# Filter spectra of a long convolution: two half-row products with a sum and a difference on GpSimd, in place of two stacked products

## The chip, the cores and the metric

The kernel runs on one core of a Trainium2 chip. The metric is the device time of one execution in microseconds; the time before is 1944.95 us, the median of three runs that went from 1944.28 to 1946.02 us. A core has TensorE (PE; its weight loads are shown apart as PEld), VectorE (DVE), ScalarE (ACT), GpSimd (POOL) and SyncE (SP, which here issues most DMAs). Each engine takes its instructions strictly in the order in which they stand in its own queue. They meet only through semaphores.

## The reference, cut to what matters

The program is a two-layer block followed by another two-layer block, 256 tokens by 1024 channels in float32. The change touches one piece of the last layer, the filters of a two-sided long convolution and their spectra:

```python
def hyena_filters(l, w1, b1, ..., freq, filt_out):
    ...
    hdn = jnp.sin(fr * (hdn @ w3.astype(f32) + b3.astype(f32)))          # 256 x 64
    h = (hdn @ filt_out.astype(f32)).reshape(l, 2, HY_ORDER, D_MODEL)    # direction, order, channel
    window = jnp.exp(-t.reshape(l, 1, 1, 1) * deltas) + HY_SHIFT
    return h * window

def long_conv(z, h_fwd, h_bwd, skip):
    l = z.shape[1]
    k = jnp.concatenate([h_fwd, jnp.zeros_like(h_fwd[:1]), jnp.flip(h_bwd[1:], axis=0)], axis=0)
    y = jnp.fft.irfft(jnp.fft.rfft(z, n=2 * l, axis=1) * jnp.fft.rfft(k, axis=0)[None], n=2 * l, axis=1)[:, :l]
    return y + z * skip.astype(jnp.float32)
```

The kernel needs the spectrum of `k` only through two combinations of the windowed filters: the even part, forward plus backward, whose cosine transform is the real part, and the odd part, forward minus backward, whose sine transform is the imaginary part. The backward filter counts from its second row on. The skip is added to the first row of the even part.

## The kernel before

Nearly all of the time goes into weight products in three passes: a weight unit `w` of 128x1024 is loaded, ACT rounds it to `wh` (L469), DVE makes the rest `wl` (L470), and TensorE runs three products for each piece (L483 to L485). The filters are side work that has no dependence on the tokens. The generator `filters` (L2032) computes them in eight steps, one for each of two orders `n` and four quarters `q` of 256 channels, and puts the spectra into the DRAM tile `spec` for the last layer.

Before the first step, `hd`, the 64x256 output of the small network, is copied into two 128-row tiles: `he` holds it twice, `ho` holds it above its negative. The backward column of the first row is zeroed in `he`. One step then

- loads the window `fwin`, the skip `fk` and the filter weights `fw`, in which the forward weights stand in rows 0 to 63 and the backward weights in rows 64 to 127,
- makes the even part with `he` and the odd part with `ho`, each as two products of 128 rows by 128 columns against 256 columns (L2061) into a bank of PSUM called `mm`, and multiplies each with the window on DVE into `fb` (L2064); the sum over 128 rows adds or subtracts the two directions,
- adds the skip to one row of the even part on POOL (L2066),
- makes four products with the transform matrix `H` (L2071), two for the even rows of time (j = 0) and two for the odd rows (j = 1), copies the first pair to `fe` on ACT (L2075), and makes `fs` as their sum and `fe` as their difference on DVE (L2077, L2078), which two DMAs write to `spec`.

In float32 each of these products appears in the trace as two passes. All tiles of a step have one buffer, so a step's `fb` is free only when the step before has read it. There are three `mm` banks, and two banks `aux2`.

In the code, six steps stand after the heads of the second block's first layer and ahead of its output projection `ab_w_out` (`self.fill(FILL)`, where one of the seven items is the set-up), and two stand in the ffn of that layer with `aux2` banks. But the program is built with a list scheduler (`schedule_with_timeline_sim=True`), which sets the order of every queue by its own estimates. It moves the six steps forward among the work of the two recurrent heads there: the inverse of the delta rule (L1712 to L1742) and its state scan (L1779 to L1822, states `dS`, output `do`), and the gates and scan of the gated linear attention (L1321 to L1462, output `lo`). Behind those scans `head_out` follows: squares on ACT (L1856), an inverse root `rsq` on POOL from `oss` (L332), the scaling of `do` and `lo` on DVE (L1866), transposes on TensorE (L1875), a product with the gate on DVE (L1877) and the split into `ydh`, `ydl` and `ygh`, `ygl`. The stream of `ab_w_out` reads those four.

Of the kernel before, what the change touches and what calls it, by code (L numbers as in the profile page):

```python
# [10 lines left out]
F32 = mybir.dt.float32  # L11
# [3 lines left out]
AF = mybir.ActivationFunctionType  # L15
OP = mybir.AluOpType
# [3 lines left out]
S = 256  # L20
# [228 lines left out]
class K:  # L249
# [1782 lines left out]
    def filters(self, lp):  # L2032
# [1 line left out]


        nc, A = self.nc, self.A
        he, ho = self.hd2
        for t in (he[:64], he[64:], ho[:64]):
            nc.sync.dma_start(t, self.hd)
        nc.vector.memset(he[64:, 0:1], 0.0)  # L2040
        nc.scalar.activation(ho[64:], self.hd, AF.Copy, scale=-1.0)
        nc.sync.dma_start(self.Hm, A["dft_h"])
        yield
        fo = A["hy_filt_out_2"][0]
        sh = [128, 2, 256]
        for n in range(2):
            for q in range(4):
# [3 lines left out]
                sk = lp.tile([128, 256], F32, tag="fk", name="fk")[0:1, :]  # L2051
                nc.sync.dma_start(sk, A["hy_skip_2"][0, n:n + 1, q * 256:(q + 1) * 256])
                wt = lp.tile([128, 256], F32, tag="fw", name="fw")
                for dr in range(2):
                    c0 = dr * 2048 + n * 1024 + q * 256
                    nc.sync.dma_start(wt[64 * dr:64 * dr + 64, :], fo[:, c0:c0 + 256])
                eo = []
                for i in range(2):
                    ps = self.mm()
                    for m in range(2):  # L2060
                        nc.tensor.matmul(ps[:, m * 256:(m + 1) * 256], self.hd2[i][:, m * 128:(m + 1) * 128], wt,  # L2061
                                         start=True, stop=True)
                    t = lp.tile(sh, F32, tag=f"fb{i}", name="fb")
                    nc.vector.tensor_tensor(t, ps.rearrange("p (m n) -> p m n", m=2), win, OP.mult)  # L2064
                    if i == 0:
                        nc.gpsimd.tensor_tensor(t[0:1, 0, :], t[0:1, 0, :], sk, OP.add)  # L2066
                    eo.append(t)
                for j in range(2):
                    ps = self.mm()
                    for i, t in enumerate(eo):  # L2070
# [135 lines left out]
    def run(self, stages=("b1l0", "b1l1", "b2l0", "b2l1", "fin")):  # L2206
# [18 lines left out]
        if "b2l1" in stages:  # L2225
            fm = es.enter_context(self.pool("fm", "right"))
            self.Fm = fm.tile([128, 512], F32, name="F")
            self.Gm = fm.tile([128, 4, 128], F32, name="G")
            self.Hm = fm.tile([128, 512], F32, name="H")
            self.hd2 = [fm.tile([128, S], F32, name=f"hd{i}") for i in range(2)]  # L2230
            self.spec = self.dr.tile([128, 4, 4 * 512], F32, name="spec")
        if "b2l0" in stages:
            if "b1l1" not in stages:
# [39 lines left out]
```

## Time and profile before

| | |
|---|---|
| median of three runs | 1944.95 us |
| profiled execution | 1944.3 us |
| its span in the trace | 1942.5 us |
| PE busy | 1905.6 us, 98% of the span |
| DVE busy | 1479.6 us, 76% |
| ACT busy | 1050.7 us, 54% |
| POOL busy | 119.0 us, 6% |
| mean granted clock of TensorE | 0.994 |

The span is the time between the first and the last instruction in the trace; 1.8 us of the execution lie outside it. Busy time is the union of an engine's instructions. PE runs its passes into one another, so the distance between the starts of two passes, not the length of one, says how fast it goes. The granted clock is the share of its 2.4 GHz that TensorE was given: 1.0, or 0.5 for 1.2 GHz.

### The profile page before, as it was taken

To read this page: it belongs to the slowest core of one execution; us is meant where nothing else is said; L and a number is where in the kernel's file an instruction comes from. 1 tells how busy PE (TensorE), PEld (TensorE's weight loads), DVE (VectorE), ACT (ScalarE), POOL (GpSimd) and SP (SyncE) were. 2 spreads that over 40 slices of the span, in tenths; PEclk is the share of its full clock that TensorE was granted. 3 is DMA by queue.
4 is the path that set the end of the run, shared out by engine and by line. 5 is a ranking of instruction groups with operands and counts; after the bars stand their busy time and mean duration, and the time that the engine had idled before them with its cause. 6 is when DMAs were issued, how large, how long until landed. Compare 5 with 4: busy or idle time off the path is not lost.

```text
span 1942.5 us, 39726 instructions
## 1 busy us (share of the span) xinstructions
PE 1905.6 (98%) x16234; PEld 1859.7 (96%) x16234; DVE 1479.6 (76%) x2362; ACT 1050.7 (54%) x1642; POOL 119.0 (6%) x120
## 2 busy tenths in 40 slices
PE   7999999999999999999999999998999999999998
PEld 7999999999999999999999999997899999899998
DVE  5988987896776879977778966887775557997554
ACT  6664455564644774454555544765254446555443
POOL 0102000110001001000000000000110000010001
PEclk9999999999999999999999999999999999999999
DMA  8865755966567766756653536443146666535653
GB/s 314 290 220 196 243 188 184 308 237 215 182 226 240 266 213 206 242 166 212 244 186 117 188 115 209 150 152 112 63 153 203 195 189 208 178 112 188 193 190 123
DMA packets 118759, 379.63 MB, mean 195 GB/s; under 512 B 18755, under 2 KB 28784, under 8 KB 117296
## 3 DMA queue, kind: packets, MB, share of 16 engines
q1 hardware_dynamic: 117808, 376.44, 57.7%
q8 instruction: 127, 2.08, 0.4%
q0 software_dynamic: 768, 0.66, 0.1%
q14 instruction: 56, 0.46, 0.1%
HBM read 365.94 MB, written 10.25 MB: 194 GB/s over the span
## 4 chain that ended last, share of the span: by engine, by line
PE 88%; DVE 4%; ACT 3%; issue 2%; DMA 1%; POOL 0%; SPq 0%; DVEq 0%; POOLq 0%; ACTq 0%
PE mm L485 23%; PE mm L483 23%; PE mm L484 23%; DVE wl L470 1%; ACT wh L469 1%; PE mm L519 1%; PE aux L1224 1%; PE mm L520 1%; PE mm L521 1%; PE aux L2123 1%; PE aux L2106 1%; PE aux L859 1%; DMA mw<-in_t_mod_w 1%; PE aux L483 1%; PE aux L485 1%
## 5 line engine op out<-in xcount | busy, mean ns | idle before, releaser
L469 ACT CAST wh<-w 128x1024 fp32r<-128x1024 f32 (+2 forms) x570 | 589.0, 1035 | 626.9 <-PE mm L484 473.6
L470 DVE TENSOR_TENSOR wl<-w,wh 128x1024 fp32r<-128x1024 f32 (+2 forms) x570 | 684.4, 1202 | 280.3 <-ACT wh L469 277.7
L483 PE MATMUL mm<-hh,wh 128*128 128x256 f32 (+1 forms) x1776 | 499.9, 282 | 1.4 <-ACT bq L766 0.7
L485 PE MATMUL mm<-hh,wl 128*128 128x256 f32 (+1 forms) x1776 | 499.4, 282 | 1.2 <-DVE wl L470 1.0
L484 PE MATMUL mm<-hl,wh 128*128 128x256 f32 (+1 forms) x1776 | 498.5, 281 | 0.0
L485 PEld LDWEIGHTS mm<-hh,wl 128*128 128x128 f32 (+1 forms) x1776 | 332.6, 187 | 4.1 <-DVE wl L470 1.8
L483 PEld LDWEIGHTS mm<-hh,wh 128*128 128x128 f32 (+1 forms) x1776 | 332.7, 187 | 3.5 <-issue 1.0
L484 PEld LDWEIGHTS mm<-hl,wh 128*128 128x128 f32 (+1 forms) x1776 | 332.3, 187 | 2.4 <-issue 1.8
L485 PE MATMUL mm<-xh,wl 128*128 128x256 f32 x960 | 269.6, 282 | 1.5 <-DVE wl L470 1.5
L483 PE MATMUL mm<-xh,wh 128*128 128x256 f32 x960 | 267.9, 280 | 1.2 <-DVE dqT L1262 0.7
L484 PE MATMUL mm<-xl,wh 128*128 128x256 f32 x960 | 268.6, 281 | 0.2
L485 PE MATMUL mm<-ph,wl 128*128 128x256 f32 x704 | 196.4, 279 | 0.0
L483 PE MATMUL mm<-ph,wh 128*128 128x256 f32 x704 | 195.9, 278 | 0.0
L484 PE MATMUL mm<-pl,wh 128*128 128x256 f32 x704 | 195.8, 278 | 0.0
L485 PEld LDWEIGHTS mm<-xh,wl 128*128 128x128 f32 x960 | 181.1, 189 | 5.1 <-issue 2.6
L483 PEld LDWEIGHTS mm<-xh,wh 128*128 128x128 f32 x960 | 180.8, 189 | 4.1 <-issue 2.7
L484 PEld LDWEIGHTS mm<-xl,wh 128*128 128x128 f32 x960 | 180.6, 189 | 2.9 <-issue 2.2
L1218 DVE SCALAR_TENSOR_TENSOR macc<-mw,cs,macc 128x512 f32<-128x512 f32 x196 | 145.6, 747 | 14.0 <-DMA mw<-in_t_mod_w 13.1
L484 PEld LDWEIGHTS mm<-pl,wh 128*128 128x128 f32 x704 | 132.4, 188 | 0.0
L485 PEld LDWEIGHTS mm<-ph,wl 128*128 128x128 f32 x704 | 132.2, 188 | 0.1
L483 PEld LDWEIGHTS mm<-ph,wh 128*128 128x128 f32 x704 | 132.1, 188 | 0.0
L483 PE MATMUL mm<-brh,wh 128*128 128x256 f32 x384 | 107.9, 281 | 0.0
(705 smaller groups left out, 3478.6 us busy)
## 6 DMA issues: line engine op xcount, KB each, us to landing
w<-in_t_w_in SPq DMA_DIRECT2D x148, 512.0 KB
w<-in_t_ffn_w SPq DMA_DIRECT2D x128, 512.0 KB
mw<-in_t_mod_w SPq DMA_DIRECT2D x96, 512.0 KB
w<-in_t_ffn_w_up SPq DMA_DIRECT2D x88, 512.0 KB
w<-in_t_ab_w_in SPq DMA_DIRECT2D x42, 512.0 KB
w<-in_t_ffn_w_down SPq DMA_DIRECT2D x40, 512.0 KB
w<-in_t_w_lift SPq DMA_DIRECT2D x32, 512.0 KB
w<-in_t_hy_w_in SPq DMA_DIRECT2D x24, 512.0 KB
```

Of the source, the lines that this page charges most:

```text
L469: nc.scalar.copy(wh, w)
L470: nc.vector.tensor_tensor(wl, w, wh, OP.subtract)
L483: nc.tensor.matmul(ps, wh, xh, start=start, stop=False)
L484: nc.tensor.matmul(ps, wh, xl, start=False, stop=False)
L485: nc.tensor.matmul(ps, wl, xh, start=False, stop=stop)
L519: nc.tensor.matmul(o, h, wh, start=(k + tb == 0), stop=False)
L520: nc.tensor.matmul(o, h, wl, start=False, stop=False)
L521: nc.tensor.matmul(o, l, wh, start=False, stop=(k == KT - 1 and tb == 1))
L859: nc.tensor.matmul(ps[:, jj * S:jj * S + ns], qr[r, 2 * jp + jj, tb * 128:(tb + 1) * 128], kr[r, 0, :ns], start=True, stop=True)
L1218: nc.vector.scalar_tensor_tensor(acc, v[:, k, :], sc, acc, op0=OP.mult, op1=OP.add)
L1224: nc.tensor.matmul(ps[:, m:m + 1], acc[:, m * 128:(m + 1) * 128], self.ones[:, :1], start=True, stop=True)
L2106: nc.tensor.matmul(ps, self.Fm[:, c0:c0 + 128], zt[:, part, :], start=True, stop=True)
```

## The change

In each step the two directions are computed apart. The forward rows of `fw` meet rows 0 to 63 of `he`, the backward rows meet rows 64 to 127, in turns (`m` outside, `r` inside), each into a PSUM bank of its own. Both banks are multiplied with the window. Then POOL makes the difference into a new tile `fo`, the sum in place, and the skip as before. `ho` and what filled it (one DMA, one ACT instruction) go away.

```diff
-        he, ho = self.hd2
-        for t in (he[:64], he[64:], ho[:64]):
+        he = self.he
+        for t in (he[:64], he[64:]):
             nc.sync.dma_start(t, self.hd)
         nc.vector.memset(he[64:, 0:1], 0.0)
-        nc.scalar.activation(ho[64:], self.hd, AF.Copy, scale=-1.0)
...
-                eo = []
-                for i in range(2):
-                    ps = self.mm()
-                    for m in range(2):
-                        nc.tensor.matmul(ps[:, m * 256:(m + 1) * 256], self.hd2[i][:, m * 128:(m + 1) * 128], wt,
+
+                fb = []
+                pd = [self.mm() for _ in range(2)]
+                for m in range(2):
+                    for r in range(2):
+                        p = slice(64 * r, 64 * r + 64)
+                        nc.tensor.matmul(pd[r][:, m * 256:(m + 1) * 256], self.he[p, m * 128:(m + 1) * 128], wt[p, :],
                                          start=True, stop=True)
-                    t = lp.tile(sh, F32, tag=f"fb{i}", name="fb")
+                for r, ps in enumerate(pd):
+                    t = lp.tile(sh, F32, tag=f"fb{r}", name="fb")
                     nc.vector.tensor_tensor(t, ps.rearrange("p (m n) -> p m n", m=2), win, OP.mult)
-                    if i == 0:
-                        nc.gpsimd.tensor_tensor(t[0:1, 0, :], t[0:1, 0, :], sk, OP.add)
-                    eo.append(t)
+                    fb.append(t)
+                odd = lp.tile(sh, F32, tag="fo", name="fo")
+                nc.gpsimd.tensor_tensor(odd, *fb, OP.subtract)
+                eo = [fb[0], odd]
+                nc.gpsimd.tensor_tensor(eo[0], *fb, OP.add)
+                nc.gpsimd.tensor_tensor(eo[0][0:1, 0, :], eo[0][0:1, 0, :], sk, OP.add)
                 for j in range(2):
```

The scheduler also orders the queues anew. Line numbers shift: L2061 becomes L2062, the window product L2064 becomes L2066, difference, sum and skip on POOL are L2069, L2071 and L2072, the products with `H` L2071 become L2076, the copy L2075 becomes L2080, and sum and difference on DVE L2077 and L2078 become L2082 and L2083. In the rows that follow, numbers tell buffers apart; the two directions of a step write different `mm` banks, so two numbers in turns are two row halves in turns.

On PE, the fourth step's products among the scan of the delta rule. Before, the fifth step's products at the same place of the scan:

```order
L2061 MATMUL mm_17047<-fw_17044,hd0_14869 128x256 x2
L1392 MATMUL aux_16670<-lf_16634 128x64 x4
L1392 MATMUL aux_16671<-lf_16634 128x64 x4
L2061 MATMUL mm_17053<-fw_17044,hd1_14870 128x256
L1806 MATMUL aux_15978<-du0_15946,dkd_15945 128x128 x4
```

Now, the fourth step's:

```order
L2076 MATMUL mm_17006<-fo_16998,H_14868 128x256
L2062 MATMUL mm_17022<-fw_17019,hd_14869 128x256 x2
L1806 MATMUL aux_15977<-du0_15945,dkd_15944 128x128 x4
L1779 MATMUL aux_15986<-dS1_15953,dkT_15171 128x128 x4
L1788 MATMUL aux_15996<-dS1_15953,dqT_15316 128x128 x4
L1406 MATMUL aux_16681<-lla_16608,cst_72 128x256 x2
L2062 MATMUL mm_17023<-fw_17019,hd_14869 128x256 x2
L1800 MATMUL aux_16002<-drhs_15991,dY_15192 128x128 x4
```

The scheduler has pulled the turns apart: both products of one direction stand together, and work of the whole array stands between the directions. So it is in steps four, seven and eight; in steps three and six the directions follow each other as two blocks of two; only in steps one, two and five do they stand in turns, as the code writes them.

On PE, the last stretch ahead of the stream of `ab_w_out` (L483 to L485 with `ydh`). Before, from the end of the scans (L1437, L1439) through the transposes of `do` and `lo` (L1875):

```order
L1437 MATMUL aux_16739<-lS1_16697,le31_16619 128x256
L1439 MATMUL aux_16739<-lv_16390,lAT1_16648 128x128 x2
L1875 MATMUL aux_16183<-cst_72,do_15951 128x128
L1875 MATMUL aux_16254<-cst_72,do_15951 128x128
L1875 MATMUL aux_16183<-cst_72,do_15951 128x128 x3
L1875 MATMUL aux_16254<-cst_72,do_15951 128x128 x3
L1875 MATMUL aux_16828<-cst_72,lo_16692 128x128
L1875 MATMUL aux_16899<-cst_72,lo_16692 128x128
L483 MATMUL mm_17100<-ydh_16094,wh_17102 128x256
```

Now, from the last two transposes of `lo` on; the four products of the fifth step (in turns) stand directly behind the last L1439, ahead of the transposes of `do`:

```order
L1875 MATMUL aux_16827<-cst_72,lo_16691 128x128 x3
L1875 MATMUL aux_16898<-cst_72,lo_16691 128x128 x3
L2076 MATMUL mm_17070<-fb_17062,H_14868 128x256
L2076 MATMUL mm_17070<-fo_17066,H_14868 128x256
L2076 MATMUL mm_17074<-fb_17062,H_14868 128x256
L2076 MATMUL mm_17074<-fo_17066,H_14868 128x256
L2062 MATMUL mm_17090<-fw_17087,hd_14869 128x256 x2
L2062 MATMUL mm_17091<-fw_17087,hd_14869 128x256 x2
L2076 MATMUL mm_17104<-fb_17096,H_14868 128x256
L2076 MATMUL mm_17104<-fo_17100,H_14868 128x256
L2076 MATMUL mm_17108<-fb_17096,H_14868 128x256
L2076 MATMUL mm_17108<-fo_17100,H_14868 128x256
```

All products of the fifth and sixth step, which stood among the scans, now stand between the scans and the stream, whose first L483 is the next row. In the sixth step the products with `H` follow the products that they need with nothing between.

On POOL, the same place. Before, from the last memset of the inverse to the squares of the next norm (L364):

```order
L1690 MEMSET dT 128x1024
L2066 TENSOR_TENSOR fb<-fb,fk 1x256 x6
L332 TENSOR_TENSOR rsq<-oss,cst 128x4 x4
L364 TENSOR_TENSOR sq<-sq 128x256 x5
L332 TENSOR_TENSOR rsq<-ms,cst 128x2
```

Now, from the fourth step's skip on, with the numbers:

```order
L2072 TENSOR_TENSOR fb_17028<-fb_17028,fk_17017 1x256
L332 TENSOR_TENSOR rsq_16104<-oss_16095,cst_72 128x4
L332 TENSOR_TENSOR rsq_16115<-oss_16095,cst_72 128x4
L2069 TENSOR_TENSOR fo_17066<-fb_17062,fb_17064 128x512
L332 TENSOR_TENSOR rsq_16753<-oss_16746,cst_72 128x4
L332 TENSOR_TENSOR rsq_16761<-oss_16746,cst_72 128x4
L2071 TENSOR_TENSOR fb_17062<-fb_17062,fb_17064 128x512
L2072 TENSOR_TENSOR fb_17062<-fb_17062,fk_17051 1x256
L2069 TENSOR_TENSOR fo_17100<-fb_17096,fb_17098 128x512
L2071 TENSOR_TENSOR fb_17096<-fb_17096,fb_17098 128x512
L2072 TENSOR_TENSOR fb_17096<-fb_17096,fk_17085 1x256
```

The fifth step's difference stands between the two pairs of inverse roots of `head_out`, the rest of steps five and six behind them. On DVE, the fifth step's two window products (L2066) stand between the scalings of the two halves of `do` (L1866); its sum and difference and the sixth step's window products follow behind the last split of `head_out`.

## Rows read from the trace of the kernel before

**Rows 1.** The page: span; busy time, share, instructions; the chain that ended last.

```profile
span 1942.5 us, 39726 instructions
PE 1905.6 (98%) x16234; PEld 1859.7 (96%) x16234; DVE 1479.6 (76%) x2362; ACT 1050.7 (54%) x1642; POOL 119.0 (6%) x120
...
PE 88%; DVE 4%; ACT 3%; issue 2%; DMA 1%; POOL 0%; SPq 0%; DVEq 0%; POOLq 0%; ACTq 0%
```

**Rows 2.** Windows: stretch, its us, PE, PEld, DVE, ACT, POOL busy, clock, DMA.

```profile
1315.50:1397.00 81.50, 75.15 (x774) 66.22 (x772) 58.73 (x123) 31.84 (x61) 4.41 (x6) 0.96 0.30 97
1321.00:1327.90 6.90, 5.72 (x34) 4.31 (x31) 4.57 (x7) 6.26 (x9) 0.58 (x1) 0.51 0.40 117
1397.00:1405.40 8.40, 4.45 (x20) 3.52 (x19) 6.90 (x18) 5.45 (x24) 4.31 (x4) 0.65 0.00 0
1405.40:1409.80 4.40, 4.40 (x22) 4.40 (x21) 2.89 (x6) 1.24 (x2) 0.00 (x0) 0.50 0.02 4
1409.80:1470.00 60.20, 59.95 (x483) 58.86 (x483) 46.11 (x69) 35.04 (x59) 7.84 (x8) 1.00 0.55 170
```

**Rows 3.** Lines of a step: duration ns min/median/max, first and last start, form.

```profile
L2061 PE MATMUL mm<-fw,hd x48: 378/379/634, 1315.5 to 1379.1; 128*128 128x256 f32 x48
L2064 DVE TENSOR_TENSOR fb<-mm,fwin x12: 652/682/692, 1320.1 to 1380.3; 128x512 f32<-128x512 f32 x12
L2066 POOL TENSOR_TENSOR fb<-fb,fk x8: 711/717/2040, 1320.9 to 1458.4; 1x256 f32<-1x256 f32 x8
```

**Rows 4.** Timeline of PE: start, us, line, array rows*columns, shape, passes [idle before].

```profile
1324.50 2.93 PE L2071 MATMUL mm<-fb,H 128*128 128x256 f32 x6 [1.18 <-ACT osg L1870]
...
1350.81 1.89 PE L2071 MATMUL mm<-fb,H 128*128 128x256 f32 x8
1352.54 1.03 PE L2061 MATMUL mm<-fw,hd 128*128 128x256 f32 x4
```

**Rows 5.** The same; the first row is a window of 0.03 us alone.

```profile
1336.32 0.33 PE L1392 MATMUL aux<-lf 64*128 64x64 f32 x2
...
1336.32 1.11 PE L1392 MATMUL aux<-lf 64*128 64x64 f32 x16
1337.36 1.13 PE L2071 MATMUL mm<-fb,H 128*128 128x256 f32 x4
1338.42 1.06 PE L1718 MATMUL aux<-dT,dY 64*64 64x32 f32 x15
```

**Rows 6.** A POOL group by line and form: count, busy us, mean ns, idle before.

```profile
L1690 POOL MEMSET dY<- 128x2048 f32 x2 | 3.6, 1812 | 21.3 <-PE mm L484 11.4 <-PE aux L1558 9.9
```

**Rows 7.** Timelines of POOL and DVE beside each other; then two lines of DVE.

```profile
1416.35 0.75 POOL L364 TENSOR_TENSOR sq<-sq 128x256 f32<-128x256 f32 x1 [13.25 <-ACT sq L361]
1420.62 1.89 POOL L364 TENSOR_TENSOR sq<-sq 128x256 f32<-128x256 f32 x2 [3.52 <-ACT sq L361]
...
1420.93 1.86 DVE L396 SCALAR_TENSOR_TENSOR ul<-xT,gains,uh 128x256 fp32r<-128x256 f32 x2
...
L396 DVE SCALAR_TENSOR_TENSOR ul<-xT,gains,uh x24: 471/754/969, 1167.7 to 1751.9; 128x256 fp32r<-128x256 f32 x24
L1506 DVE TENSOR_TENSOR ivt<-ivw x28: 412/420/427, 1074.0 to 1311.2; 128x256 f32<-128x256 f32 x28
```

**Rows 8.** Timelines from the scans to the stream: PE, then DVE, then POOL.

```profile
1396.45 0.61 PE L1439 MATMUL aux<-lv,lAT 128*128 128x128 f32 x4
1399.51 0.62 PE L1875 MATMUL aux<-cst,do 128*128 128x128 f32 x2 [2.45 <-DVE do L1866]
...
1405.40 0.56 PE L484 MATMUL mm<-ydl,wh 128*128 128x256 f32 x1
...
1398.67 0.69 DVE L1866 TENSOR_TENSOR do<-do,rsq 128x512 f32<-128x512 f32 x1
...
1400.46 0.69 DVE L1866 TENSOR_TENSOR do<-do,rsq 128x512 f32<-128x512 f32 x1
...
1398.91 2.29 POOL L332 TENSOR_TENSOR rsq<-oss,cst 128x4 f32<-128x4 f32 x2 [0.72 <-ACT ojunk L1856]
```

More of the change, by code (lines that the diff above doesn't have):

```diff
@@ L2229, in run @@
             self.Hm = fm.tile([128, 512], F32, name="H")
-            self.hd2 = [fm.tile([128, S], F32, name=f"hd{i}") for i in range(2)]
+            self.he = fm.tile([128, S], F32, name="hd")
             self.spec = self.dr.tile([128, 4, 4 * 512], F32, name="spec")
```

## Prediction

> **What bounds the kernel now.** I read the page first. PE is busy 98% of the span and holds 88% of the chain that ended last [rows 1]; the weight stream sets the pace, and side work counts where it takes PE's time or keeps PE waiting. The windows show the one place where that differs. From 1315.5 us, the first filter product, to 1397.0, the end of the scans, PE is busy 75.15 of 81.50 us. From 1397.0 to 1405.4 it is busy 4.45 of 8.40 us: the outputs of the heads wait for squares, inverse roots and scalings. From 1405.4 on PE never waits, but until 1409.8 the granted clock is 0.50, and only then 1.00 [rows 2]. So a filter step inside the scans fills PE there, and whatever stands between the last scan product and the stream pushes all that follows.
>
> **Products of the two directions.** A pass of the whole array against 256 columns takes (1352.54 - 1350.81)/8 = 0.216 us at full clock [rows 4], although each one's listed length, with its tail, is 379 ns [rows 3]. Eight passes, 1.73 us, make both directions of a step. With 64 rows, the trace shows that two passes on different row halves run beside each other: in L1392, whose code writes the halves in turns, two start within 0.03 us, and 16 passes take 1337.36 - 1336.32 = 1.04 us, eight pairs of 0.13 [rows 5]. In turns a step would thus take about 4 x 0.216 = 0.86 us and save 0.86. Against it stand the changes between whole and half array: four whole passes between half ones take 1338.42 - 1337.36 = 1.06 us in place of 0.86 [rows 5], so a way there and back costs 0.20, one change 0.10.
>
> But the order of the queues gives turns only in steps one, two and five. Steps one and two, with one extra change each, save 0.75 each. Step three in blocks overlaps only where the blocks meet, 0.216 - 0.10 = 0.1. Step four stands in two places among whole-array work, saves nothing and pays 0.40. Up to the end of the scans this makes 0.75 + 0.75 + 0.1 - 0.4 = **1.2 us** saved. Steps seven and eight, split in the same way inside the weight stream, lose 0.40 each, **0.8 us**. Here the Trainium skill (TensorEngine Tiling (Array Packing), Theoretical Speedup) speaks of up to 2x for a contraction of 64 or less. By that alone eight steps would give 8 x 0.86 = 6.9 us; by the rows and the order the eight save less than 1 us outside the tail.
>
> **Sum and difference on POOL.** No row of before has a 128x512 sum there. One of 128x256 takes 0.75 us, two in a row 1.89 [rows 7]; the skip, one partition by 256, takes 0.717 [rows 3], so columns set the price, not partitions. Doubled, 0.75 gives 1.50 at most. A memset grows by 1.81 us over 2048 columns [rows 6], 0.23 us for 256 more: 0.96 at least. I take 1.35, nearer to the sum, since that has two inputs. A step's chain on POOL was 0.72 and becomes 1.35 + 1.35 + 0.72 = **3.4 us** (2.6 to 3.7). Two of DVE's L396 beside two POOL sums took 1.86 us where one alone takes 0.47 [rows 7]: DVE instructions with two inputs from SBUF wait for the POOL instruction to end, and POOL waits for them, so each of the new sums can hold DVE up by as much as 1.35. The skill (GPSIMD Engine Reference, 4.1 Engine selection) sends an elementwise pair to VectorE, GpSimd being about twice as slow with two inputs; 0.75 against 0.42 for L1506 agrees [rows 7]. By that rule the pair would cost 2 x 0.68 on DVE, and each exposed chain would be 1.3 us shorter.
>
> **The stretch of the scans.** Before, all six steps stood in it; now four do. Two steps of 8 + 8 passes leave: 32 x 0.216 = 6.9 us. With the 1.2 us saved, the scans could end 8.1 us earlier if PE sets their pace. It does mostly (75.15 of 81.50, rows above), but the removed filler also covered the scan's own chain (product, copy, product, update), and the eight new sums of steps one to four hold up DVE, whose part of the chain they can meet. I take **-7** (bounds -8.1 and -4.5).
>
> **From the scans to the stream.** Set the end of the last L1439 to 0, 1396.9 us in before; the stream then began at 8.5 [rows 8]. Now, step by step:
> - Half of `do` is scaled by 2.46 (1398.67 + 0.69) [rows 8]. Then DVE makes the fifth step's two window products, 2 x 0.68 [rows 3]; POOL's difference of 1.35 follows, ahead of two inverse roots. `head_out` is pushed by up to 2.7; DVE waited 1400.46 - 1399.36 = 1.1 us for ACT and POOL in the same place [rows 8], which absorbs part, so 1.6 to 2.7 remain. Two passes of the stream, 0.2 each (22 in 4.40 us [rows 2]), no longer stand among the transposes, which then end at 8.5 + 1.6 - 0.4 = 9.7 to 10.8. I take 10.5.
> - The fifth step's `H` products, eight passes: 1.73 us at full clock, or 0.43 each and 3.46 at half clock; six in 2.93 us, with the tail, at clock 0.51 show that [rows 2, 4]. PE idles in pieces here as it did before, where the clock fell, so I take 3.46.
> - The sixth step's products, one block after the other, seven passes long where the blocks meet: 1.5 us, or 3.0 at half clock. Beside them DVE makes `fs` and `fe` (each as long as a window product), then the window products, the last of them behind the last pass: 4 x 0.68 = 2.7, or 3.0 + 0.68 = 3.7, which I take.
> - POOL's chain with PE waiting: 3.4 (2.6 to 3.7).
> - The sixth step's `H` products: 1.73 to 3.46; I take 3.46, after 3 to 5 us of idle PE.
>
> Sum: 10.5 + 3.46 + 3.7 + 3.4 + 3.46 = 24.5, bounds 9.7 + 1.73 + 2.7 + 2.6 + 1.73 = 18.5 and 10.8 + 3.46 + 3.7 + 3.7 + 3.46 = 25.1. The stream begins **16.0** us later behind the scans (10.0 to 16.6). It lost 2.2 us to the clock before (4.40 us at 0.50); part of this loss now falls on the `H` products, so I give back 0.7 (0 to 2.2).
>
> **The two steps in the ffn.** Besides the 0.8 us of array changes, the `H` products stand some 70 passes behind their inputs, 8 us, and the chain there (window product, 3.4 on POOL, waits of up to 1.2 for each wl on DVE) takes 5 to 9. DVE is busy 46.11 of 60.20 us there [rows 2], with a margin. I take 1.3 in all (0.5 to 4).
>
> The removed ACT instruction and DMA lie far ahead of this, where ACT and the queue have slack: 0. On SP, the sixth step's two stores to `spec` wait longer and stand ahead of one weight load, which itself waits for a buffer that the stream frees: 0.
>
> **Sum.** -7 + 16.0 - 0.7 + 1.3 = +9.6 us. The profiled execution took 1944.3, 0.65 below the median; by the median, 1944.95 + 9.6 = 1954.55, **1954.6 us**. Ends: -8.1 + 10.0 - 2.2 + 0.5 = +0.2, and -4.5 + 16.6 + 4 = +16.1.
>
> **Rivals.**
> - *The clock stays at 1.00 through the tail* (not slower). The products of step five, the transposes and the fifth `H` products now stand where PE idled for 2.45 us; if that keeps the clock up, `H` products and blocks take 1.73, 1.5 and 1.73, and the stream needs no recovery: 10.5 + 1.73 + 2.7 + 3.4 + 1.73 - 8.5 = 11.6 later, less 2.2, less 7.5, plus 0.8 = +2.7, 1947.6. For it: the fall before came only after more than two idle microseconds. Against: PE still waits three times in the tail. It decides where the stream begins before 21 us at full clock. Chance 0.20.
> - *PE sets every price* (faster): the two directions overlap wherever they stand beside other work, DVE fills early and the sixth chain hides behind `head_out`. Then 8 x 0.56 (0.86 less three changes) saved gives 1940.5. The 2x above would be this case. Against it stands the order, in which nothing is between the sixth step's products. Chance 0.06.
> - *DVE becomes the bound in the ffn*: 6.8 us of POOL work there hold DVE, which is busy for three quarters, and late weight splits stop PE for 5 us more: 1959.5. Chance 0.12. The forecast itself has 0.62.
>
> **How the numbers follow.** About 0.2%, 3.9 us, is what a measurement of this kernel can tell from no change. Slower by more: forecast and DVE case, 0.74. Within: the clock rival, 0.20. Faster: 0.06. The range runs from the low end of the sum to its high end, 1945 to 1961; outside it lie the faster case and part of the extremes.
>
> **What would show it.** Right: L1439 ends near 1390, the first `ydh` product of the stream near 1415; PE waits over 4 us ahead of the last four L2076, released by POOL; the clock is 0.5 at the sixth step; L2062 shows overlapping starts only in steps one, two and five. Wrong: POOL's 128x512 sums well under 1 us; a clock of 1.00 between 1395 and 1415; scans that end at 1396 as before, since then the scan's own chain sets their pace and I am too low; or waits at L2076 of the ffn.

## The result, and the profile after

The changed kernel takes 1968.84 us (median of four runs, 1967.2 to 1971.0); the kernel before, beside it, 1945.49 (1944.28 to 1948.18). The ratio is 1.0113, with an interval of 1.0100 to 1.0126: it is 23.4 us slower. I had said slower, by 9.6 us, in a range that ended at 1961: the sign was right, the size and the range were not. The profiled execution took 1971.0 us.

The page of the changed kernel, with the same columns as [rows 1]:

```profile
span 1968.9 us, 39753 instructions
PE 1916.9 (97%) x16234; PEld 1867.5 (95%) x16234; DVE 1489.4 (76%) x2362; ACT 1050.5 (53%) x1641; POOL 143.9 (7%) x136
...
PE 88%; DVE 4%; ACT 3%; issue 2%; DMA 1%; POOL 0%; SPq 0%; DVEq 0%; POOLq 0%; ACTq 0%
```

The page hardly differs. PE is busy 11 us longer in a span that is 26 us longer; POOL, which got 24 us of sums, still shows 7%. To find the loss one has to go by stages. Four marks cut the program: the first filter product, the last L1439 (the end of the scans), the start of the weight stream, the end of PE's work. (Before, two passes of the stream already stand among the transposes, from 1403.6 us on; the mark is its unbroken run from 1405.4 on.) Each stretch against that of the kernel before:

| stretch | before, us | after, us | difference | predicted |
|---|---|---|---|---|
| start to first filter product | 1315.5 | 1320.8 | +5.3 | 0 |
| to the end of the scans | 81.4 | 85.4 | +4.0 | -7 |
| to the stream | 8.5 | 25.4 | +16.9 | +16.0 |
| stream to the end | 530.2 | 530.1 | -0.1 | -0.7 + 1.3 |

The first line is most likely scatter and not the change: ahead of the first filter product the work differs only by the one ACT instruction and the one DMA that filled `ho`. In the changed kernels below this product started between 1316.9 and 1321.1 us, and in the two other kernels that still fill `ho` at 1319.3 and 1320.1. The other three lines add up to +20.8 us of the 23.4. The third came 0.9 us above the forecast, just beyond its upper bound of 16.6. The fourth is 0.7 below, less than this stretch scatters by. The second is where the forecast failed, by 11 us.

The windows of that stretch in the changed kernel, cut where the granted clock changes (columns as in [rows 2]; the last but two is the clock):

```profile
1320.79:1326.46 5.67, 2.27 (x40) 1.71 (x39) 5.23 (x11) 5.59 (x10) 0.00 (x0) 1.00 0.53 181
1326.46:1346.94 20.48, 18.58 (x195) 16.55 (x192) 12.42 (x17) 9.10 (x14) 4.62 (x3) 0.50 0.13 40
1346.94:1367.40 20.46, 16.89 (x270) 14.65 (x268) 16.98 (x28) 8.98 (x16) 7.14 (x6) 1.00 0.34 103
1367.40:1374.25 6.85, 5.61 (x28) 4.96 (x30) 3.31 (x8) 0.00 (x0) 0.12 (x1) 0.50 0.11 41
1374.25:1406.20 31.95, 30.85 (x220) 27.81 (x218) 20.73 (x54) 6.76 (x19) 3.25 (x3) 1.00 0.17 55
sum 85.41, PE 74.19 PEld 65.68 DVE 58.67 ACT 30.43 POOL 15.13; mean PE 14.84 PEld 13.14 DVE 11.73 ACT 6.09 POOL 3.03
```

The same stretch before, and its one window at 0.50:

```profile
1315.49:1396.90 81.41, 75.06 (x774) 66.22 (x772) 58.64 (x123) 31.75 (x60) 4.41 (x6) 0.96 0.30 97
1321.05:1327.88 6.83, 5.65 (x32) 4.24 (x29) 4.55 (x7) 6.21 (x9) 0.53 (x1) 0.50 0.40 118
```

Before, that window was 6.83 us with PE busy 5.65. Now there are two, 20.48 and 6.85 us, with PE busy 18.58 + 5.61 = 24.2. At half clock, half of the busy time is loss: 2.8 us before, 12.1 now, **+9.3**. PE stood idle 81.4 - 75.1 = 6.3 us before and 85.4 - 74.2 = 11.2 now, **+4.9**. What is left, PE's work as it would be at full clock, fell from 72.2 to 62.1 us, **-10.1**. Together +4.1, which is the +4.0. The split is good to about 1 us: a kernel below with the same work on PE shows -9.0 by it. So the work that I wanted out of the stretch, 8.1 us, did leave it; the clock and the waiting took more than it gave.

Where the waits are, from the timeline of PE (start, us, line, shapes, passes, and in brackets the idle time before and who ended it):

```profile
1328.07 0.81 PE L1380 MATMUL aux<-le,le2w 64*128 64x128 f32 x4 [1.21 <-DVE le L1360]
...
1336.40 1.97 PE L1392 MATMUL aux<-lf 64*128 64x64 f32 x16
1338.30 1.22 PE L2076 MATMUL mm<-fb,H 128*128 128x256 f32 x2
...
1368.64 2.07 PE L1779 MATMUL aux<-dS,dkT 128*128 128x128 f32 x8 [4.32 <-DMA dS<-std]
```

Two things are to be seen. The first `H` products of step one stand at 1338.3, 17.5 us behind the step's first product, with some 10 us of half- and quarter-array work (64 rows) ahead of them; before, they began 6.6 us behind it, the last six passes at [rows 4], and the clock rose just behind those. And the scan of the delta rule waits 4.32 us for its first state `dS`; the clock's second fall comes within that wait. The queue of SP shows what stands ahead of its load:

```profile
1361.38 0.37 SPq L2086 DMA_DIRECT2D spec<-fs  x1
1362.10 0.37 SPq L2086 DMA_DIRECT2D spec<-fe  x1
1362.64 1.11 SPq L2055 DMA_DIRECT2D fw<-in_hy_filt_out  x2
1363.86 0.52 SPq L2048 DMA_DIRECT2D fwin<-in_window  x1
1364.56 0.82 SPq L1768 DMA_DIRECT2D dS<-std  x2
```

The state loads stand behind the stores of step two and the loads for step four. What the queue waited for between 1352 and 1366 us, the view of its waits says (us in total, times, longest; its largest entry):

```profile
SPq L2086 <- DVE fs L2082: 4.4, 1, 4.4
```

It waited 4.4 us for DVE's sum `fs` of step two, which ended at 1361.35; from then on it issued one DMA behind the other. The window tile `fwin` has a single buffer, but DVE had read it for step three by 1363.3, before its load had its turn at 1363.9, and the view lists no wait of that load. In the kernel before, the same two state loads were issued here, ahead of the filter's loads:

```profile
1356.07 0.84 SPq L1768 DMA_DIRECT2D dS<-std  x2
1357.01 0.47 SPq L2056 DMA_DIRECT2D fw<-in_hy_filt_out  x1
```

Counted from the first filter product, the first state load is issued at 40.6 us before and at 43.8 now. Of these 3.2 us, 1.9 are the filter's loads ahead of it; the rest is that the stores themselves come later.

### The profile page after: what moved, and what is told of

Its sections match the earlier page's. It is cut to its first block, busy times and chain, and to the rows that moved or that the text cites. A ratio compares the mean times of both kernels' runs of the same rounds, so it can differ in the third digit from the quotient of the medians.

```text
span 1968.9 us, 39753 instructions
## 1 busy us (share of the span) xinstructions
PE 1916.9 (97%) x16234; PEld 1867.5 (95%) x16234; DVE 1489.4 (76%) x2362; ACT 1050.5 (53%) x1641; POOL 143.9 (7%) x136
## 4 chain that ended last, share of the span: by engine, by line
PE 88%; DVE 4%; ACT 3%; issue 2%; DMA 1%; POOL 0%; SPq 0%; DVEq 0%; POOLq 0%; ACTq 0%
PE mm L485 23%; PE mm L483 23%; PE mm L484 23%; PE mm L519 1%; PE mm L520 1%; PE mm L521 1%; DVE wl L470 1%; ACT wh L469 1%; PE aux L1224 1%; PE mm L2076 1%; DMA mw<-in_t_mod_w 1%; PE aux L2128 1%; PE aux L2111 1%; PE aux L859 1%; PE aux L483 1%
## 5 line engine op out<-in xcount | busy, mean ns | idle before, releaser
L483 PE MATMUL mm<-hh,wh 128*128 128x256 f32 (+1 forms) x1776 | 500.6, 282 | 1.4 <-ACT bq L766 0.7
L485 PE MATMUL mm<-hh,wl 128*128 128x256 f32 (+1 forms) x1776 | 500.1, 282 | 1.6 <-DVE wl L470 1.5
L485 PEld LDWEIGHTS mm<-hh,wl 128*128 128x128 f32 (+1 forms) x1776 | 333.3, 188 | 4.5 <-DVE wl L470 2.6
L483 PEld LDWEIGHTS mm<-hh,wh 128*128 128x128 f32 (+1 forms) x1776 | 333.4, 188 | 3.4 <-issue 1.0
L485 PE MATMUL mm<-xh,wl 128*128 128x256 f32 x960 | 268.8, 281 | 1.5 <-DVE wl L470 1.5
L483 PE MATMUL mm<-xh,wh 128*128 128x256 f32 x960 | 267.6, 280 | 1.1 <-DVE dqT L1262 0.7
L485 PE MATMUL mm<-ph,wl 128*128 128x256 f32 x704 | 196.6, 279 | 0.0
L483 PE MATMUL mm<-ph,wh 128*128 128x256 f32 x704 | 196.0, 278 | 0.0
L485 PEld LDWEIGHTS mm<-xh,wl 128*128 128x128 f32 x960 | 181.0, 189 | 4.9 <-issue 2.6
L483 PEld LDWEIGHTS mm<-xh,wh 128*128 128x128 f32 x960 | 180.7, 189 | 3.9 <-issue 2.7
L485 PEld LDWEIGHTS mm<-ph,wl 128*128 128x128 f32 x704 | 132.2, 188 | 0.2
L483 PEld LDWEIGHTS mm<-ph,wh 128*128 128x128 f32 x704 | 132.1, 188 | 0.0
L483 PE MATMUL mm<-brh,wh 128*128 128x256 f32 x384 | 107.9, 281 | 0.0
```

What stands on the lines that cost most here:

```text
L483: nc.tensor.matmul(ps, wh, xh, start=start, stop=False)
L485: nc.tensor.matmul(ps, wl, xh, start=False, stop=stop)
```

## The experiments

My theory after this reading: the tail is what I forecast (two steps deferred, POOL's chain open before PE); the 11 us in the scans are (a) a longer half clock, because the early whole-array products are gone, and (b) the state loads, which a filter load in front of them now holds up. The rivals: half-row products are dear by themselves; POOL's latency alone is all of it; the scans are bound by their own chain. The experiments ran on other chips than the first runs. There the kernel before took 1948.9 to 1950.7 us (medians), and the time of one kernel scattered by 5 us and more, so ratios go against the kernel before on the same chip, and the stretches of the traces, which repeat far better, decide.

**The changed kernel again.** No edit; the base of the others.

> The changed kernel itself, on the chip of the other experiments, as their base. Theory: 18 to 24 us above the kernel before, with the stretch from first filter product to last L1439 near 85 us, a wait of 4 us at L1779 on dS, a half clock of 20 us early in the scans and the stream 25 us behind them. If chance made the first profile what it was, one of the three long items (20 us half clock, 4 us wait, 25 us tail) is absent here.

Measured: 1973.0 us, ratio 1.0110 (1.0080 to 1.0141). Stretch 85.3 us, wait at L1779 4.4, 20.5 us at half clock, stream 25.4 us behind the last L1439 started. All three items are the kernel's, not chance.

**The state loads on another queue.**

```diff
-                nc.sync.dma_start(sd.rearrange("p a b -> p (a b)"), self.std[:, d, :])
+                nc.scalar.dma_start(sd.rearrange("p a b -> p (a b)"), self.std[:, d, :])
```

and the same for L1426.

> The changed kernel with the scans' state loads (L1768, L1426) issued on ScalarE's DMA queue in place of SyncE's, where the first pair stood behind a window load that waits for its buffer; every other engine's queue is the same. Theory (the wait of 4.3 us at L1779 on dS and the 6.8 us at half clock behind it are lost time): the wait goes, the stretch falls from 85 to 78 to 81 us, and the time by 4 to 7 us, to 1962 to 1965 us. Rival (the chain of the scans waits at the next place instead): the stretch stays at 84 to 85, the time within 1.5 us of the changed kernel's.

Measured: 1967.1 us, ratio 1.0090 (1.0069 to 1.0111), above the 1962 to 1965 expected. That alone doesn't part it from the changed kernel. The trace does. L1779 no longer waits, and the second half-clock window is gone:

```profile
1363.81 0.33 PE L1382 MATMUL aux<-le,le2w 64*128 64x64 f32 x2
1364.07 1.16 PE L1779 MATMUL aux<-dS,dkT 128*128 128x128 f32 x8
```

```profile
1320.42:1401.50 81.08, 72.51 (x741) 63.99 (x740) 58.51 (x115) 30.41 (x58) 15.16 (x12) 0.87 0.24 73
1326.50:1347.00 20.50, 18.62 (x188) 16.62 (x189) 12.36 (x16) 8.66 (x13) 4.62 (x3) 0.50 0.14 40
```

The first two rows are the timeline of PE, the others windows of the stretch and of its early half-clock part. The stretch is 81.1 us in place of 85.4: the late loads cost **4.3 us**. The buffer of the window tile, which the expectation names, had no part in it by the view of waits above; how the 4.3 us part between the stores' wait for DVE and the loads in front, this run doesn't say. Two further kernels below that keep this edit show 81.4 and 80.9. The early 20.5 us at 0.50 are untouched, so (a) and (b) are two causes.

**Four whole-array products where the H products used to stand.** Added to the kernel with the state loads moved:

```diff
+                if n == 0 and q == 0:
+                    pz = self.mm()
+                    for m in range(4):
+                        nc.tensor.matmul(pz[:, m % 2 * 256:(m % 2 + 1) * 256], self.Hm[:, m * 128:(m + 1) * 128], win[:, m % 2, :],
+                                         start=True, stop=True)
...
-                    ps = self.mm()
+                    ps = self.mm() if pz is None or j else pz
```

> The kernel of the state-load experiment (changed kernel, state loads on ScalarE's queue) with four more 128x256 products of H on the window tile in the first step, written to the bank that the first H product overwrites; in TensorE's queue they are one added group, between the first L1712 group and the first L1380, where in the kernel before the first step's own H products stand (1322 to 1326 us). Theory (with the H products gone from that place only half- and quarter-array work is left, and that is why the granted clock stays at 0.5 for 20.5 us in place of 6.8): the episode shortens to 7 to 11 us, the stretch from first filter product to last L1439 from 81.0 to 75 to 78 us, the time by 3 to 5 us against the state-load experiment. Rival (TensorE's waits, 1.3 us at L1380 and 0.5 at L1723, hold the clock down): the episode stays near 20 us and the stretch grows by 1.7 to 3.5 us.

**The same four with 64 of the 128 rows** (`self.Hm[:64, ...]`, `win[:64, ...]`), in the same place of the same queue:

> As the kernel with four early H products in the first step, with the same order of TensorE's queue, but the four added products use 64 of the 128 rows, so that they fill the same time with half of the array. Theory (whole-array products at that place are what brought the clock back): the half clock lasts 17 to 24 us again, the stretch is 80 to 84 us, some 5 us more than the 76.3 with whole-array products. Rival (that the place is filled at all, over TensorE's wait of 1.3 us, is what counts): 3 to 7 us of half clock and a stretch of 76 to 78 us.

Measured: 1961.8 us, ratio 1.0060 (1.0039 to 1.0080), with whole-array products; 1968.5, ratio 1.0092 (1.0066 to 1.0119), with half-array ones. First the whole-array kernel: its added products on PE, then windows of the stretch, of the half-clock part, and of what follows:

```profile
1326.19 3.56 PE L2067 MATMUL mm<-fwin,H 128*128 128x256 f32 x8
1329.69 0.56 PE L1380 MATMUL aux<-le,le2w 64*128 64x128 f32 x4
```

```profile
1320.13:1396.50 76.37, 68.94 (x749) 59.92 (x748) 58.16 (x115) 30.74 (x58) 15.04 (x12) 0.96 0.25 79
1326.50:1329.90 3.40, 3.40 (x10) 2.24 (x10) 3.37 (x4) 3.37 (x5) 2.79 (x2) 0.50 0.02 5
1329.90:1350.30 20.40, 18.97 (x346) 17.05 (x346) 15.46 (x25) 11.25 (x18) 5.39 (x5) 1.00 0.27 85
```

Then the half-array kernel, in the same order:

```profile
1326.03 3.78 PE L2067 MATMUL mm<-fwin,H 64*128 64x256 f32 x8
1329.60 0.80 PE L1380 MATMUL aux<-le,le2w 64*128 64x128 f32 x4
```

```profile
1319.17:1402.10 82.93, 76.20 (x749) 67.13 (x748) 58.70 (x115) 30.61 (x58) 15.13 (x12) 0.86 0.23 73
1323.50:1347.40 23.90, 23.21 (x226) 20.57 (x227) 13.74 (x19) 10.60 (x16) 4.61 (x3) 0.50 0.14 43
```

In both, PE is busy from the L1712 before until behind L1380 with no gap for DVE's `le`; the added group takes 3.56 and 3.78 us. Behind 128 rows the clock is back at 1.00 when the group ends, and stays there for 20 us before it falls once more, for 3.4 us; behind 64 rows it stays at 0.50 until 1347.4, 23.9 us in all. The stretch differs by 6.6 us. Two further kernels below have the whole-array group, and 3.4 us at half clock around it as well. The half-array group ran in one kernel, and its clock fell 2.5 us ahead of the group, in the others with the group's start. In the kernel before it fell over 3 us ahead of the six passes at [rows 4] and came back at their end all the same. So that the place is filled at all, as the rival had it, is not what counted: the products on 128 rows brought the clock back there, the same on 64 rows did not. How many it takes stays open: in the changed kernel the first four passes with `H`, on 128 rows and at half clock from 1338.3 to 1340.3, were not followed by a rise; it came at 1346.9. Against the kernel without the added products the stretch lost 4.7 us, and that net of 1.7 us that the four cost at full clock (8 passes).

**Stacked products with POOL's chain.** The kernel before, and behind its two products the changed kernel's three POOL operations:

```diff
-                    if i == 0:
-                        nc.gpsimd.tensor_tensor(t[0:1, 0, :], t[0:1, 0, :], sk, OP.add)
...
+                nc.gpsimd.tensor_tensor(eo[1], *eo, OP.subtract)
+                nc.gpsimd.tensor_tensor(eo[0], *eo, OP.add)
+                nc.gpsimd.tensor_tensor(eo[0][0:1, 0, :], eo[0][0:1, 0, :], sk, OP.add)
```

> The kernel before with its stacked whole-row products, and behind them the changed kernel's GpSimd chain (a 128x512 difference, a 128x512 sum, the skip) on the two products; the spectra are then not the reference's. Theory (GpSimd's latency makes the tail, the missing whole-row products lengthen the half clock in the scans): the scans' stretch (first filter product to last L1439) stays near 81 to 83 us, the stream begins 16 to 20 us after the last L1439 since in this queue the sixth step alone stands there, and the time is 1953 to 1960 us. Rival (GpSimd's latency alone makes the whole loss): 85 us for the stretch, 1964 to 1971 us in all.

Measured: 1957.3 us, ratio 1.0039 (1.0026 to 1.0052). The time is where I put it, the reason is not. The stretch is 85.7 us, as in the changed kernel, and the half clock lasts 23.9 us although the filter products use the whole array:

```profile
1319.32:1405.00 85.68, 78.81 (x755) 71.31 (x754) 58.02 (x117) 31.11 (x60) 17.98 (x15) 0.84 0.24 75
1323.60:1347.50 23.90, 22.04 (x222) 19.58 (x223) 13.92 (x19) 11.72 (x18) 4.62 (x3) 0.50 0.13 43
```

With POOL's chain in between, the scheduler puts the `H` products of step one behind L1380, L1723 and L1392 (first at 1336.9), and `dS` waits here too (2.9 us). The tail is 14.5 us, below the 16 to 20 expected, as only one step is deferred.

**Half-row products without the sums.** The changed kernel with `eo = fb`.

> The changed kernel's half-row products without the difference and sum, the two directions' products fed to the H products as they are (the skip stays); the spectra are then not the reference's. Theory (GpSimd's chain makes the tail; the half-row products give no shorter scans, since the scans' own waits and the half clock set that stretch): the stream begins about 8.5 us after the last L1439 as before, the stretch takes 79 to 83 us, and the time is 1941 to 1948 us. Rival 1 (each step's 0.86 us is worth its full size on TensorE): 1937 to 1940. Rival 2 (the half-row products cost by themselves, by a half clock of 20 us in place of 7): stretch 85 or more, 1949 to 1953.

Measured: 1956.0 us, ratio 1.0049 (1.0029 to 1.0069): too slow for the theory and for rival 1, by rival 2's stretch but without its mechanism. Windows of the stretch and of the early half clock, then one row of PE's timeline:

```profile
1318.81:1404.95 86.14, 77.59 (x773) 66.35 (x772) 58.07 (x120) 30.65 (x56) 4.30 (x6) 0.92 0.29 91
1324.30:1331.10 6.80, 5.47 (x24) 3.58 (x21) 4.59 (x7) 5.98 (x8) 0.32 (x1) 0.50 0.39 119
```

```profile
1365.02 1.91 PE L1779 MATMUL aux<-dS,dkT 128*128 128x128 f32 x8 [2.33 <-DMA dS<-std]
```

The early half clock is 6.8 us, as before, since the `H` products stand early again: half-row products don't bring the long one. The stream begins 9.2 us behind the start of the last L1439 (6.8 before, 25.5 in the changed kernel, by the same measure): without the sums nearly all of the tail is gone, as the theory had it. But the stretch is 86.1. Two later half-clock windows of 3.4 us cost 3.4 together, `dS` waits 2.3 us (here behind a store to `spec`), and the six steps' half-row products save next to nothing: charged by the order in which the passes end and put at full clock, they take 10.2 us where the stacked ones took 11.3, and L1800 and L1806, into which they are mixed, take 1.0 more. The scheduler moved much else in this kernel, so I take from it only that the half-row form isn't the cause of the long half clock, and that its own gain is small once it is pulled apart.

**The sums on VectorE.** `nc.vector` for `nc.gpsimd` in L2069 and L2071.

> The changed kernel with the 128x512 difference and sum on VectorE; the one-row skip stays on GpSimd. Theory (the loss is GpSimd's latency, which leaves the fifth and sixth steps behind the scans, +16 to 17 us there, and +4 in the scans): in this kernel's queue the H products of the fifth step stand inside the scans again and only those of the sixth behind them, right after their filter products, so the stream of weight products should begin some 10 to 13 us after the last L1439 (25.5 in the changed kernel, 8.5 before), and the time should be 1947 to 1956 us. Rival (the half-row products and the half clock that goes with them cost by themselves): the scans stay long, the time stays at 1960 or above.

Measured: 1956.1 us, ratio 1.0042 (1.0026 to 1.0059); the stream begins 11.8 us behind the last L1439 started. The two sums take a little over half of POOL's time:

```profile
L2069 DVE TENSOR_TENSOR fo<-fb x8: 687/692/693, 1326.6 to 1474.4; 128x512 f32<-128x512 f32 x8
```

against the changed kernel's

```profile
L2069 POOL TENSOR_TENSOR fo<-fb x8: 1261/1271/3212, 1327.5 to 1491.0; 128x512 f32<-128x512 f32 x8
```

(ns, least, median, most). Of the 1.0110 of the changed kernel, 0.7%, some 13 us, are gone: 13.6 us of tail, and 3.1 of the stretch (82.3 us, in which `dS` comes in time), less what VectorE's 11 us of sums and scatter cost elsewhere. The early half clock is still 20.5 us: the scheduler keeps the first `H` products behind L1392 in this kernel too. So the long half clock doesn't need POOL: it comes with the sums on either engine, and in both kernels the order keeps the first `H` products back. That any other operation in that place would do the same is not shown.

**The sixth step's sums alone on VectorE**, on top of the moved state loads; PE's order is the same.

> The state-load experiment with the sixth step's difference and sum on VectorE; TensorE's order is the same. Theory (TensorE's wait ahead of the sixth step's H products is the chain of difference, sum and skip itself): that chain falls from 1.26 + 1.26 + 0.71 to 0.69 + 0.69 + 0.71, so the wait falls from 5.2 to about 4.0 us and the stream begins 22.5 to 23.8 us behind the last L1439 in place of 24.3. Rival (the wait is set by something else, as the window products before the chain): no change of the wait.

Measured: 1969.3 us, ratio 1.0105 (1.0079 to 1.0132). The mechanism shows, the gain doesn't:

```profile
1417.87 1.71 PE L2062 MATMUL mm<-fw,hd 64*128 64x256 f32 x8
1423.40 1.22 PE L2077 MATMUL mm<-fb,H 128*128 128x256 f32 x2 [3.82 <-POOL fb L2073]
...
1426.62 0.78 PE L483 MATMUL mm<-ydh,wh 128*128 128x256 f32 x1
```

The wait ahead of the sixth `H` products is 3.8 us for 5.2, more than the 1.1 that the three operations got shorter. But the last L1439 started at 1401.88, so the stream still begins 24.7 us behind it, for 24.3 with the loads alone moved: the clock came back later here, at 1419.1 for 1415.2. By that the fifth step's `H` products took 3.55 us for 2.51, the sixth step's half-row products 1.71 for 1.14, and its `H` products 3.2 for 3.0, together 1.8 us more, against the 1.3 us that the wait lost. For the total the run is inconclusive.

**Two steps later.** `FILL = 5` in place of 7, on top of the moved state loads; the same with the four early products; and the kernel before with that number.

> The state-load experiment with four filter steps ahead of the weight products in place of six (FILL 5 for 7), so that the fifth to eighth steps go beside the weight products. Theory (the tail of 25.5 us is two deferred steps with GpSimd's chain exposed, and beside weight products that chain is hidden): stream 8 to 10 us after the last L1439, two steps' products (5 to 6 us of TensorE) added later, in all 9 to 12 us less than the state-load experiment, 1955 to 1958 us beside its 1967. Rival (the chain shows beside the weight products as well, some 4 us a step): less than 4 us gained, 1963 us or more.

> Both edits of the two kernels beside it: the four early whole-array products, and four filter steps ahead of the weight products. Theory: the gains add, 1951 to 1955 us. Rival (the scans are then bound by their own chain and not by TensorE): as the kernel with the later steps alone, within 1.5 us.

> The kernel before with FILL 5 for 7. Theory (in the scans TensorE sets the pace at its clock, so a step costs the same there as beside the weight products): within 3 us of the kernel before. Rival (the scans' own chain hides a part of the steps' products): 4 to 8 us slower.

Measured, in this order: 1959.6 us, ratio 1.0045 (1.0028 to 1.0063); 1954.7, ratio 1.0018 (1.0002 to 1.0033); 1953.4, ratio 1.0013 (0.9996 to 1.0030). The first lies above the 1955 to 1958 us expected. In it the stream begins 6.8 us behind the start of the last L1439, as in the kernel before by the same measure, 24.3 without the edit: the 17 us of the tail go as a whole. From there to the end it takes 539.5 us, 11 more than with the loads alone moved, of which a part is scatter: that stretch measured between 528.2 and 535.9 us in the eleven kernels with the same work in it, 532 on average, and 541.8 and 541.0 in the other two with `FILL` 5. So the two steps cost some 9 us beside the weight products, more than the 5 to 6 that I had put down. POOL's chain showed no wait of PE there, against the rival. In the second the stretch is 79.1 us for 81.4. The third says that, for the kernel before, it makes no difference that can be told. Its stretch is the plainest test of what a step taken out of the scans is worth:

```profile
1320.12:1398.10 77.98, 69.80 (x742) 61.66 (x740) 53.08 (x112) 29.66 (x54) 2.98 (x4) 0.93 0.24 77
```

With neither half-row products nor sums in it, two steps less take 6.7 us of PE's work out (72.2 to 65.5, split as above), and the scans get 3.4 us shorter, 78.0 for 81.4: PE idles 1.8 us more, and the half clock, 10.2 us of it in place of 6.8, costs 1.4 more.

**VectorE's sums, early products and moved loads together.**

> Difference and sum on VectorE (2 x 0.69 us a step), state loads on ScalarE's queue, and the four early whole-array products. Theory (early half clock, state loads and GpSimd's chain are the three parts of the loss): against the kernel with VectorE sums alone the early half clock shortens from 20.5 to 3 to 7 us and the time falls by 4 to 6, to 1949 to 1952 us, within 0.2% of the kernel before. Rival (VectorE is then the bound in the scans): less than 2 us gained, 1954 or more.

Measured: 1951.4 us, ratio 1.0010 (0.9998 to 1.0022), the stretch 77.6 us, the tail 12.2. With the three causes treated, the changed kernel's 21 us on these chips (1.0110) are down to 2, which the interval doesn't tell from nothing. No kernel that I ran is faster than the one before.

## Why the prediction failed, step by step

**The scans: the failed step.** "I take **-7** (bounds -8.1 and -4.5)" became +4.0. The sum under it was sound in its main term: PE's work at full clock fell by 9 to 10 us, against my 8.1. What failed was the step from work to time, that the scans end as much earlier "if PE sets their pace": it took over the clock and the waits of before, with 1.1 us to spare. The kernel before with `FILL` 5 lost 3.4 us of time for 6.7 of work even without the new products and sums. I had the window 1321.0 to 1327.9 at 0.51 in my rows [rows 2], and that the clock came back at its end, behind the `H` products [rows 4]; I used these rows for the price of a pass at half clock, and didn't ask what the clock would do if the order took those products away. That was worth 9.3 us: 6.5 by the early half clock, 20.5 us at 0.50 in place of 6.8, and 2.8 by the later fall within the wait for `dS`, which the next paragraph counts too. With the 4.9 us of idle time, 14.2 us stand against the 10.1 of work. Four whole-array products in the old place gave back 4.7 net; four half-array ones gave back nothing.

**The queue of SP: priced at 0, cost 4.3.** I named the two stores that wait longer in the sixth step, and passed over the state loads, which moved behind the filter's loads and behind stores that wait for DVE's `fs`. Moving the loads took 4.3 us off the stretch: 2.7 of idle time (a wait of 1.3 for POOL's `fb` at the next L2076 took part of the old one's place) and 2.8 of half clock, less 1.1 that the split above counts as work. The order shows the move, and the code that the stores need DVE's sum. Both were there to be read.

**Products of the two directions.** In turns, a step's eight passes take 1.13 us where eight whole-array ones took 1.89 [rows 4], both with the tail: 0.76 saved, and I had put down 0.75. Blocks overlap more than "only where the blocks meet": the sixth step's two blocks start in pairs, two passes within a window of 0.04 us:

```profile
1422.10 0.49 PE L2062 MATMUL mm<-fw,hd 64*128 64x256 f32 x2
...
1377.46 1.13 PE L2062 MATMUL mm<-fw,hd 64*128 64x256 f32 x4
1378.51 1.16 PE L1806 MATMUL aux<-du,dkd 128*128 128x128 f32 x8
```

The last two rows are step four, pulled apart: four passes take as long as eight in turns, so it saves nothing, as forecast. Charged as in the kernel without the sums, the first four steps' passes take 5.5 us where the stacked ones took 7.5. But L1800 and L1806, into which they are mixed, take 0.9 us more, and that leaves about 1.1 for my 1.2. The Trainium skill (TensorEngine Tiling (Array Packing), Theoretical Speedup) has up to 2x; 1.89 us against 1.13 is 1.7, in turns and in the sixth step's blocks.

**Sums on POOL.** 1.26 us alone for my 1.35, and up to 3.2 beside DVE. The Trainium skill (GPSIMD Engine Reference, 4.1 Engine selection) has two-input work about twice as slow on GpSimd; 1.26 against 0.69 agrees.

**From the scans to the stream: 25.4 for 24.5, the chain right.** The tail of the changed kernel on PE:

```profile
1417.21 1.54 PE L1875 MATMUL aux<-cst,lo 128*128 128x128 f32 x6 [0.98 <-DVE lo L1866]
1418.55 1.06 PE L2076 MATMUL mm<-fb,H 128*128 128x256 f32 x2
...
1422.10 1.14 PE L2062 MATMUL mm<-fw,hd 64*128 64x256 f32 x8
1428.39 1.22 PE L2076 MATMUL mm<-fb,H 128*128 128x256 f32 x2 [5.15 <-POOL fb L2072]
...
1431.61 0.78 PE L483 MATMUL mm<-ydh,wh 128*128 128x256 f32 x1
```

and POOL's chain beside it:

```profile
1424.95 1.26 POOL L2069 TENSOR_TENSOR fo<-fb 128x512 f32<-128x512 f32 x1 [8.95 <-DVE fb L2066]
1426.29 1.26 POOL L2071 TENSOR_TENSOR fb<-fb 128x512 f32<-128x512 f32 x1
1427.63 0.71 POOL L2072 TENSOR_TENSOR fb<-fb,fk 1x256 f32<-1x256 f32 x1
```

From 1406.2 on: transposes until 1418.55, 12.3 (10.5 predicted, the head's outputs were pushed further); fifth `H` products 3.55 at half clock (3.46); sixth products and DVE until POOL starts 2.85 (3.7, since the clock was back for them); POOL's chain 3.4 (3.4); sixth `H` products 3.2 (3.46). The order of waits is the one forecast, but the sum is partly luck: +1.8 for the transposes against -0.85 and -0.26 further on, and 25.4 lies just above my upper bound of 25.1. The rival in which the clock stays at 1.00 fell: it was 0.50 from 1411.8 to 1422.0 and from 1425.4 to 1432.3.

**Stream and ffn.** -0.1 for +0.6; the view of waits lists none of PE from 1432 to 1500 us, where both ffn steps lie, so the DVE rival fell. The difference of 0.7 is within the scatter of this stretch, so the terms -0.7 and +1.3 are neither borne out nor refuted one by one.

**What I had written would prove me wrong** was scans that end at 1396 as before, "since then the scan's own chain sets their pace". They ended later still, but not for that reason: with the clock and the loads mended the stretch came to 76.4 us, 5 below before, for 6.7 us less work by the split, the 1.7 us of added products counted in. So with the clock back most of the work taken out counts. Another sign, overlapping starts "only in steps one, two and five", failed too: step six shows them throughout, step three in part.

## What to carry to other kernels

Where side work is moved out of a stretch, look whether the granted clock rose behind that very work, and price the stretch at either level; taking products out can cost more time than they took. An operation put between two products is paid less by its length than by where the scheduler then places the second one: read the new place of every product, and of every load that shares a queue with the moved ones. A store that waits for an engine's result holds up the loads behind it in the same queue, which may have nothing to do with it.

## What the runs showed of the hardware

The granted clock went back to 1.00 behind 3.6 us of products on 128 rows (three kernels), and not behind 3.8 us of products on 64 rows in the same place (one kernel), with PE busy throughout in both; four passes on 128 rows, 2.0 us, were not followed by a rise in the changed kernel either. Half-row products issued as two blocks, one direction after the other, still ran beside each other in the sixth step, 1.14 us for eight passes. A 128x512 sum took 1.26 us on POOL and 0.69 on DVE.
